# Sample window values in three transfers, and a ring of six value-page pairs, in a hybrid decoder step on Trainium2

## The chip, the cores and the metric

The kernel runs on one core of one Trainium2 chip. The metric is the device time of one execution in microseconds (us); lower is better. Engines are named as in the profile: PE (TensorE matmul), PEld (its weight loads), DVE (VectorE), ACT (ScalarE), POOL (GpSimd) and SP (SyncE, which here does nothing but issue DMA transfers).

## The reference, cut to what matters

One decoder layer runs on a prompt of 512 tokens and on 8 sample sequences of one new token each. Half of the heads do sparse attention in three branches (compressed, selected blocks, sliding window), the other half differential attention. For the samples, keys and values of 2048 past tokens lie in 16 pages of 128 tokens per sequence, found through a page table. The sliding branch of a sample has its own buffer of 512 past rows; the new token's row is appended, the oldest falls out, and the updated buffer is an output:

```python
kw = jnp.concatenate([win_k, wk], axis=1)
vw = jnp.concatenate([win_v, wv], axis=1)
w_pos = P - wbuf + jnp.arange(wbuf + Q, dtype=jnp.int32)
o = _nsa_branches(q, q_rot, gate, q_pos, kc, vc, cmp_end, n_sel, sel_gather, kw, vw, w_pos)
return o, kw[:, -wbuf:], vw[:, -wbuf:]
```

The sample's attention output is a sum over its pages of weights times values (128 tokens x 640 value columns a page: 512 for the differential heads, 128 for the selected branch), plus the compressed and the sliding branch. Then follow the output projection, a convolutional FFN and the final norm.

## The kernel before

The middle of the program (306 to 477 us of the profiled execution) is attention. Generators, one for each activity, yield operations with an estimated cost, and a planner in the kernel's Python (`Issue`) lays them in one order for each engine: at every step it takes, among the operations that could start soonest, the most urgent one by a plan that eight rehearsals refine. A number that a generator yields by itself is a pause: its next operation may not start earlier. The planner counts a transfer's result as usable 2.0 us after its end, and each ring of buffers as one more condition. Its order is fixed when the program is built; on the chip every engine runs its own instructions in that order and waits by semaphores. All transfers go through SP's one queue.

These generators matter here:

- `p_main` runs the prompt's attention in 12 units: `p_qk` (scores on PE, L423), `p_exp` (row minimum on DVE at L1828, exponential on ACT into tiles `p0` to `p3` of 128 to 512 columns), `p_scale`, `p_turn` (transposes on PE at L1889), `p_parts` (copies into `pt`) and `p_pv`. The tiles `p0` to `p3` lie in rings of `NPR` buffers each.
- `p_vload` fetches the samples' value pages in 64 pairs (`vp`, 320 KB a page, issued at L523) into a ring of `NV` pairs. `p_v` consumes them on PE: for each sample 8 pairs against `Sd` and `Ss`, then the sliding branch (`kcT` against `Sw`), then the next sample. A pair's buffer comes free when the `Ss` products of its group of two pairs are done.
- `p_win` brings the sliding branch's values of sample b into half of the tile `kcT` (two samples alternate): the whole 128 x 4 x 128 block (L2036), in which the last row holds a value that isn't wanted; then the new row from `vn` over row 127 of its last quarter (L2038), which marks `E("win", b)`; then the store of the updated buffer (L2040). `p_v` waits for `E("win", b)` before it goes on to sample b + 1, and the load for sample b waits until sample b - 2 is done.

Out-projection, FFN (up from 510 to 790 us) and the down-projection follow in straight loops.

Of the kernel before, what the change touches and what calls it, by code (L numbers as in the profile page):

```python
# [412 lines left out]
def build(tc, T, plan, last):  # L413
    with tc.manual_schedule():
        _build(tc, T, plan, last)


def _build(tc, T, plan, last):
    nc = tc.nc
    te, ve, se, ge, sy = nc.tensor, nc.vector, nc.scalar, nc.gpsimd, nc.sync  # L420
# [4 lines left out]
    def act(out, in_, func=AF.Copy, **kw):  # L425
        se.activation(out=out, in_=in_, func=func, **kw)  # L426
# [20 lines left out]
    def flat(ap):  # L447
        return ap.rearrange("p a b -> p (a b)")
# [231 lines left out]
    def E(*key):  # L680
        return ev.setdefault(key, Event())
# [979 lines left out]
    def p_window():  # L1661
# [17 lines left out]
                       t[:, j * 128:(j + 1) * 128], b4 == 0, b4 == 3)  # L1679
            yield (("pe", 0.24, f), E("wm", b)) + ((ksl,) if b == 0 else ())  # L1680
        yield ("act", tact(256), lambda: act(flat(Sw), box["p"][:, 0:256])), ksl.done, E("Sw")
    NV = 5
    PL = {}


# [83 lines left out]
    def at(*args):  # L1769
        return PL["AT"](*args)  # L1770
# [1 line left out]


    PTR, DV, WR, TMP = Ring(6), Ring(2), Ring(4), Ring(1)
    NPR = (5, 5, 5, 5)
    PR = [Ring(n) for n in NPR]
    VS = Ring(NV)
    PB, PT, W, O = {}, {}, {}, {}
    wslots, vslots = {}, {}

    def v_load(i):
        t = PL["VR"]("vp", [128, 2, 640], F32, NV)
        for n in range(2):
            page(t[:, n], T["vpg"], 128 + 2 * i + n)
        vslots[i] = t
# [29 lines left out]
    def p_exp(i, g, qs, box, sl, wslot):  # L1815
# [4 lines left out]
        for q in qs:  # L1820
# [4 lines left out]
            def f():  # L1825
                if q == 0 and g == 0:
                    W[i] = at("w", [128, 6, 4], F32, 4)
                ve.tensor_tensor_reduce(out=x, in0=x, in1=cm[:, S - n:], scale=-SC, scalar=3e38, op0=OP.add, op1=OP.min,  # L1828
                                        accum_out=W[i][:, g, q:q + 1])
            yield (("dve", tdve(n), f, PS),) + ((wslot,) if first and q == 0 else ())  # L1830
        for q in qs:
# [4 lines left out]
            def f():  # L1836
                t = at(f"p{q}", [128, n], F32, NPR[q])
                act(t, xs[q], AF.Exp, bias=W[i][:, g, q:q + 1], scale=-1.0, accum_out=W[i][:, 2 + g, q:q + 1])
# [187 lines left out]
    def win(b):  # L2026
        return kcT[:, 4 * (b % 2):4 * (b % 2) + 4]

    def p_win():

        yield E("kcT", 1)
        yield E("vn")
        for b in range(B):
            if b > 1:
                yield E("vb", b - 2)
            yield ("dma", 0.75, lambda: sy.dma_start(out=win(b), in_=T["winv"][b])),  # L2036
            yield 5.0
            yield ("dma", 0.05, lambda: sy.dma_start(out=win(b)[127:128, 3], in_=vn[b:b + 1, 0])), E("win", b)  # L2038
            yield 4.0
            yield ("dma", 0.75, lambda: sy.dma_start(out=T["swv"][b], in_=win(b))),  # L2040

    def p_v():
# [115 lines left out]
    def p_wo_first():  # L2158
# [12 lines left out]
        for m in range(2):  # L2171
            slots = [VS.slot() for _ in range(2)]
            for sl in slots:
                yield sl
                sl.got.t = -50.0
            h, l = prep["o", m] = [PL["VR"]("vp", [128, 2, 640], F32R, NV).rearrange("p a b -> p (a b)")[:, 0:1024]
                                   for _ in range(2)]
# [64 lines left out]
    for f, prio in ((p_stage2(), 0), (p_load(), 0), (p_w1v(), 0), (p_split(), 1), (p_product(), 3), (p_group("k"), 2), (p_group("v"), 2), (p_scores(), 2), (p_wload(), -1), (p_window(), 1),  # L2242
                    (p_turned(), 5), (p_vn(), 5), (p_nsa(0), 1), (p_nsa(1), 1), (p_cmp_sample(0), 1),
                    (p_cmp_sample(1), 1), (p_switch(), 0), (p_outs(), -3),
                    (p_vload(), 0), (p_win(), -1), (p_main(), 3),
                    (p_values(), 2), (p_pc(), 2), (p_seq(p_scale, range(NU)), 1),
                    (p_seq(p_turn, range(NU)), 1), (p_seq(p_pv, range(NU)), 0),
                    (p_seq(p_dv, [i for i in range(NU) if units[i][0] == "d"]), 3),
                    (p_seq(p_finish, [i for i in range(NU) if units[i][0] != "s"]), 1), (p_v(), v_prio),
                    (p_wo_first(), 4),  # L2250
                    (p_wo(), 4),
                    (p_out(0, 0, VB, "v"), 7)):
        Q.spawn(f, prio)
# [296 lines left out]
```

## Time and profile before

| | us |
|---|---|
| median of 3 runs | 950.04 (948.54 to 950.15) |
| the profiled execution's own time | 948.83 |
| its span, first to last instruction | 947.1 |
| share of the span in which PE is busy | 96% |
| attention with value pages being loaded | 329.6 to 461 |

The profile is of one execution, 1.2 us below the median of the runs; 1.7 us of its time lie outside the span. A busy PE isn't a PE at its peak: matmuls overlap, and their ends are modelled. An idle time in brackets names the event that ended it.

### The profile page before, as it was taken

The numbers are of one execution on the slowest core, as the hardware profiler recorded it, in microseconds if no ns is written. First come the engines' busy times: TensorE is split into PE (matmuls) and PEld (weight loads), VectorE is DVE, ScalarE is ACT, GpSimd is POOL, SyncE is SP. The second block draws the span as 40 slices with busy tenths as digits, with TensorE's granted clock in tenths as the row PEclk, the third lists the DMA queues.
The fourth block names the chain that finished last, engine by engine and source line by source line (L and its number), as shares of the span: only waits on it lengthen the run. The fifth ranks groups of instructions, "written<-read, shape, count | busy, mean of one in ns | idle before, by whom it ended". The sixth has DMA issues, their size and how long they took to land.

```text
span 947.1 us, 22410 instructions
## 1 busy us (share of the span) xinstructions
PE 911.7 (96%) x8628; PEld 813.8 (86%) x8628; DVE 579.2 (61%) x1396; ACT 383.9 (41%) x801; POOL 281.3 (30%) x377
## 2 busy tenths in 40 slices
PE   8999999999999889999998999999999999999995
PEld 5998888799999655655568999999999999999995
DVE  7786663356777766758854357777777777421234
ACT  5275422355555556545552234444444333211220
POOL 4120210000111000000105656666666666313230
PEclk9999999999999999999989999999999999999998
DMA  7669999977673698889714422222222222433322
GB/s 258 233 221 339 354 350 337 338 261 246 222 242 118 223 341 322 322 301 339 262 61 147 157 78 90 89 90 90 90 89 90 90 90 84 139 108 107 111 73 91
DMA packets 86059, 179.82 MB, mean 190 GB/s; under 512 B 10049, under 2 KB 28994, under 8 KB 85954
## 3 DMA queue, kind: packets, MB, share of 16 engines
q1 hardware_dynamic: 85954, 178.41, 54.7%
q8 instruction: 68, 1.11, 0.5%
q14 instruction: 37, 0.30, 0.1%
HBM read 165.78 MB, written 12.59 MB: 188 GB/s over the span
## 4 chain that ended last, share of the span: by engine, by line
PE 64%; DVE 19%; ACT 7%; issue 5%; DMA 4%; SPq 1%; POOL 1%; DVEq 0%; ACTq 0%; POOLq 0%
PE bank L423 60%; DVE c L435 12%; ACT c L426 4%; PE bank L1889 2%; DMA vp<-in_vpg 2%; DVE u L438 2%; DVE h L438 1%; DVE hl L432 1%; ACT hh L426 1%; ACT wh L426 1%; DMA kcT<-vn 1%; DMA cp<-in_cpg 1%; SPq L523 1%; POOL wl L432 0%; DVE rsm L435 0%
## 5 line engine op out<-in xcount | busy, mean ns | idle before, releaser
L423 PE MATMUL bank<-gh,wl 128*128 128x260 f32 x704 | 200.9, 285 | 3.3 <-POOL wl L432 3.3
L423 PE MATMUL bank<-gh,wh 128*128 128x260 f32 x704 | 199.1, 283 | 0.0
L423 PE MATMUL bank<-gl,wh 128*128 128x260 f32 x704 | 199.1, 283 | 0.0
L432 POOL TENSOR_TENSOR wl<-wr,wh 128x1024 fp32r<-128x1024 f32 x53 | 127.0, 2397 | 162.0 <-ACT wh L426 162.0
L426 ACT ACTIVATE wh<-wr 128x1024 fp32r<-128x1024 f32 (+2 forms) x95 | 97.2, 1023 | 157.5 <-PE bank L423 125.5
L435 DVE SCALAR_TENSOR_TENSOR c<-u,cvw,c 128x536 f32<-128x536 f32 x88 | 122.3, 1390 | 59.0 <-ACT c L426 57.4
L423 PEld LDWEIGHTS bank<-gh,wl 128*128 128x128 f32 x704 | 132.5, 188 | 6.9 <-POOL wl L432 6.9
L423 PEld LDWEIGHTS bank<-gl,wh 128*128 128x128 f32 x704 | 132.6, 188 | 0.0
L423 PEld LDWEIGHTS bank<-gh,wh 128*128 128x128 f32 x704 | 132.3, 188 | 0.1
L423 PE MATMUL bank<-xh,wh 128*128 128x260 f32 (+1 forms) x368 | 105.5, 289 | 1.1 <-ACT wh L426 1.1
L423 PE MATMUL bank<-xl,wh 128*128 128x260 f32 (+1 forms) x368 | 104.4, 286 | 1.7 <-DVE xl L435 1.6
L432 DVE TENSOR_TENSOR wl<-wr,wh 128x1024 fp32r<-128x1024 f32 (+2 forms) x41 | 52.7, 1285 | 81.0 <-ACT wh L426 80.1
L423 PE MATMUL bank<-xh,wl 128*128 128x260 f32 x352 | 100.0, 284 | 0.0
L423 PE MATMUL bank<-hh,wh 128*128 128x260 f32 (+2 forms) x340 | 96.4, 283 | 0.0
L423 PE MATMUL bank<-hl,wh 128*128 128x260 f32 (+2 forms) x340 | 96.1, 283 | 0.0
L423 PE MATMUL bank<-hh,wl 128*128 128x260 f32 (+2 forms) x340 | 96.1, 283 | 0.0
L423 PEld LDWEIGHTS bank<-xh,wh 128*128 128x128 f32 (+1 forms) x368 | 68.8, 187 | 6.8 <-issue 4.5
L423 PEld LDWEIGHTS bank<-xl,wh 128*128 128x128 f32 (+1 forms) x368 | 68.8, 187 | 2.7 <-DVE xl L435 2.7
L423 PEld LDWEIGHTS bank<-xh,wl 128*128 128x128 f32 x352 | 66.9, 190 | 0.0
L432 DVE TENSOR_TENSOR wl<-cp,wh 128x256 fp32r<-128x256 f32 x126 | 47.2, 433 | 28.8 <-ACT wh L426 27.4
L423 PEld LDWEIGHTS bank<-hh,wh 128*128 128x128 f32 x340 | 64.1, 189 | 0.0
L423 PEld LDWEIGHTS bank<-hh,wl 128*128 128x128 f32 x340 | 64.1, 188 | 0.0
(389 smaller groups left out, 1984.9 us busy)
## 6 DMA issues: line engine op xcount, KB each, us to landing
vp<-in_vpg SPq DMA_DIRECT2D x128, 320.0 KB, 5.4
kp<-in_kpg SPq DMA_DIRECT2D x128, 256.0 KB, 5.2
cp<-in_cpg SPq DMA_DIRECT2D x128, 192.0 KB, 4.2
wr<-in_w_up SPq DMA_DIRECT2D x44, 512.0 KB, 3.2
wr<-in_w_in SPq DMA_DIRECT2D x21, 512.0 KB, 5.1
wr<-in_w_down SPq DMA_DIRECT2D x16, 512.0 KB, 3.5
out_zT<-z SPq DMA_DIRECT2D x14, 260.0 KB, 5.5
wr<-in_w_down SPq DMA_DIRECT2D x8, 384.0 KB, 3.1
```

Of the source, the lines that this page charges most:

```text
L423: te.matmul(out, l, r, start=start, stop=stop)
L426: se.activation(out=out, in_=in_, func=func, **kw)
L432: eng.tensor_tensor(out=out, in0=a, in1=b, op=OP.subtract)
L435: ve.scalar_tensor_tensor(out=out, in0=a, scalar=s, in1=b, op0=o0, op1=o1, **kw)
L438: eng.tensor_tensor(out=out, in0=a, in1=b, op=op)
L523: sy.dma_start(out=dst, in_=src[bass.ds(numbers[k][i - k], 1)].rearrange("o p f -> (o p) f"))
L1889: te.transpose(p[:, j * 128:(j + 1) * 128], PB[i, g, q][0][:, k * 128:(k + 1) * 128], ident)
```

## The change

Three edits. The ring of value pages gets six pairs instead of five (5 KB more of each partition), and the ring of `p3`, the 512-column tile, four buffers instead of five (2 KB less). In `p_win` the load leaves out the last row: one transfer for the first three quarters of the block (128 rows of 1.5 KB), one for the first 127 rows of the last quarter (512 bytes each), and the new row goes out right behind them as a third, without the pause of 5.0 and in one operation that the planner takes to cost 1.2. The pause ahead of the store is 12.0 instead of 4.0. Since the planner orders everything by these figures, the order of all engines in attention is laid anew.

```diff
-    NV = 5
+    NV = 6
...
-    NPR = (5, 5, 5, 5)
+    NPR = (5, 5, 5, 4)
...
-            yield ("dma", 0.75, lambda: sy.dma_start(out=win(b), in_=T["winv"][b])),
-            yield 5.0
-            yield ("dma", 0.05, lambda: sy.dma_start(out=win(b)[127:128, 3], in_=vn[b:b + 1, 0])), E("win", b)
-            yield 4.0
+            w = win(b)
+
+            def f():
+                sy.dma_start(out=w[:, 0:3], in_=T["winv"][b][:, 0:3])
+                sy.dma_start(out=w[0:127, 3], in_=T["winv"][b][0:127, 3])
+                sy.dma_start(out=w[127:128, 3], in_=vn[b:b + 1, 0])
+            yield ("dma", 1.2, f), E("win", b)
+            yield 12.0
             yield ("dma", 0.75, lambda: sy.dma_start(out=T["swv"][b], in_=win(b))),
```

## Rows read from the trace of the kernel before

**Rows 1.** The page of the whole execution: busy time by engine, then PE and the DMA engines in 40 equal slices of the span, in tenths.
```profile
PE 911.7 (96%) x8628; PEld 813.8 (86%) x8628; DVE 579.2 (61%) x1396; ACT 383.9 (41%) x801; POOL 281.3 (30%) x377
...
PE   8999999999999889999998999999999999999995
...
DMA  7669999977673698889714422222222222433322
```

**Rows 2.** Stretches of attention: start and end, length, busy us of each engine (and instructions), granted clock, mean busy share of the 16 DMA engines, GB/s.
```profile
306.00:329.60 23.60, 21.16 (x209) 15.63 (x208) 17.93 (x71) 13.71 (x46) 0.48 (x1) 0.93 0.66 228
329.60:461.00 131.40, 125.18 (x1759) 77.07 (x1749) 93.55 (x352) 69.40 (x215) 6.01 (x7) 0.99 0.91 322
461.00:477.00 16.00, 13.71 (x159) 9.15 (x159) 13.60 (x55) 10.57 (x28) 5.29 (x4) 0.90 0.56 191
...
335.00:345.00 10.00, 9.17 (x140) 5.20 (x144) 8.98 (x36) 7.35 (x28) 1.50 (x2) 1.00 1.03 391
```

**Rows 3.** What PE waited for from 329.6 to 461 us (releaser, us in total, times, the longest), and from PE's order of time the instruction after the longest of these waits: start, length, what, count, in brackets the idle time ahead of it and what ended it.
```profile
PE bank L423 <- DMA vp<-in_vpg: 5.1, 8, 1.5
...
350.70 0.43 PE L423 MATMUL bank<-vp,Sd 128*32 128x128 f32 x8 [1.53 <-DMA vp<-in_vpg]
```

**Rows 4.** The granted clock in the two stretches of attention that follow an idle time of PE (columns as in rows 2).
```profile
350.99:354.41 3.42, 3.42 (x40) 2.29 (x29) 0.00 (x0) 1.65 (x4) 0.00 (x0) 0.50 1.06 407
473.87:480.69 6.82, 5.71 (x23) 3.54 (x23) 6.02 (x27) 6.10 (x17) 1.82 (x2) 0.50 0.16 57
```

**Rows 5.** What SP's queue waited for from 329 to 462 us: issuing line, releaser, us in total, times, the longest.
```profile
SPq L523 <- PE bank L423: 36.3, 24, 6.4
SPq L2040 <- DMA kcT<-vn: 7.4, 4, 2.3
...
SPq L2038 <- DMA kcT<-in_winv: 1.9, 3, 0.9
```

**Rows 6.** SP's issues in order of time: start, length of the group, line, transfer, count. The first five pairs and the first window load, then parts of the cycles of samples 0, 1 and 4.
```profile
306.42 0.88 SPq L523 DMA_DIRECT2D vp<-in_vpg  x2
...
309.08 4.33 SPq L523 DMA_DIRECT2D vp<-in_vpg  x8
...
322.62 0.42 SPq L2036 DMA_DIRECT2D kcT<-in_winv  x1
329.65 7.41 SPq L523 DMA_DIRECT2D vp<-in_vpg  x12
...
347.44 0.42 SPq L2040 DMA_DIRECT2D out_swv<-kcT  x1
348.44 0.88 SPq L523 DMA_DIRECT2D vp<-in_vpg  x2
349.42 0.49 SPq L2036 DMA_DIRECT2D kcT<-in_winv  x1
...
398.38 0.42 SPq L2036 DMA_DIRECT2D kcT<-in_winv  x1
...
401.52 8.83 SPq L523 DMA_DIRECT2D vp<-in_vpg  x12
410.39 0.56 SPq L2038 DMA_DIRECT2D kcT<-vn  x1
```

**Rows 7.** PE around the sliding branch's products (`kcT`,`Sw`) of sample 4, as the second row of rows 3.
```profile
417.01 0.30 PE L423 MATMUL bank<-kcT,Sw 128*32 128x128 f32 x1 [0.30 <-DMA kcT<-vn]
```

**Rows 8.** DMA in 329.6 to 461 us: packets; the queue's packets, MB and share of 16 engines; issues with KB each and median us to landing.
```profile
DMA packets 19140, 42.33 MB, mean 322 GB/s; under 512 B 2317, under 2 KB 2317, under 8 KB 19119
...
q1 hardware_dynamic: 19119, 42.04, 89.9%
...
vp<-in_vpg SPq DMA_DIRECT2D x118, 320.0 KB, 5.4
out_swv<-kcT SPq DMA_DIRECT2D x7, 256.0 KB, 4.8
kcT<-in_winv SPq DMA_DIRECT2D x7, 256.0 KB, 4.4
z<-in_w_out SPq DMA_DIRECT2D x1, 256.0 KB, 4.0
kcT<-vn SPq DMA_DIRECT2D x8, 0.5 KB, 5.9
```

**Rows 9.** DMA in 225 to 300 us, where most transfers have rows of 1.5 KB: the queue's packets, MB and share of 16 engines.
```profile
q1 hardware_dynamic: 10565, 15.03, 62.0%
```

**Rows 10.** The exponentials of 512 columns as a group (ACT, 320 to 480 us: count, busy us, mean ns, idle ahead of them), then the two on ACT and the two turns on PE that stand closest.
```profile
L426 ACT ACTIVATE p<-bank,w 128x512 f32<-128x512 f32 x24 | 16.4, 685 | 16.6 <-DVE w L1828 13.6 <-DVE w L1850 2.9
...
391.72 0.68 ACT L426 ACTIVATE p<-bank,w 128x512 f32<-128x512 f32 x1
...
392.60 0.69 ACT L426 ACTIVATE p<-bank,w 128x512 f32<-128x512 f32 x1
...
392.02 0.55 PE L1889 MATMUL bank<-cst,p 128*128 128x128 f32 x3
...
393.29 0.98 PE L1889 MATMUL bank<-cst,p 128*128 128x128 f32 x7
```

**Rows 11.** PE at the end of attention, as the second row of rows 3.
```profile
473.50 0.74 PE L557 MATMUL bank<-cst,rsm 128*128 128x128 f32 x4 [1.18 <-DVE w L1850]
...
475.57 1.09 PE L1889 MATMUL bank<-cst,p 128*128 128x128 f32 x4 [1.06 <-DVE t L435]
```

## The prediction

> **What bounds the kernel now.** I read the page first, then attention by stretches, then what PE and SP wait for in it, then the transfers. The page shows PE busy nearly from end to end, and the one place with both PE and the DMA engines near their limit: slices 14 to 20, attention with value pages [rows 1]. By stretches, 329.6 to 461 us has PE busy 125.2 of 131.4 us and each DMA engine busy 0.91 of the time; what follows needs few transfers [rows 2]. So PE sets the time, and only its idle time and its slow clock can be won back; the DMA engines are the runner-up, with some 13 us to spare in 131.
>
> In that stretch PE stands idle 6.2 us. 5.1 of these end with the landing of a value page, in eight places, the longest 1.53 us ahead of 350.70 [rows 3]. Right behind that one the granted clock is 0.50, the lower of the two levels (1.2 GHz), for 3.4 us from 350.99; it is so again for 6.8 us from 473.87, where PE waits on DVE [rows 4]. At half the clock 3.4 us of matmuls do 1.7 us of work, so the wait at 350 may have cost up to 1.7 us more.
>
> SP waits 36.3 us for PE to free page buffers, 7.4 for the new row to land ahead of the store, and 1.9 for the load to land ahead of the row [rows 5]. Its order of issues shows why the sliding branch matters: for sample 4 the load goes out at 398.38, but the row only at 410.39, behind twelve page issues of the sort that wait for buffers [rows 6]. PE reaches sample 4's sliding product and waits the last 0.30 us for that row, at 417.01, 6.6 us after its issue [rows 7]. Only then does `p_v` go on to sample 5. So pages are held until the row is there, then eaten in a burst, and the ring runs dry behind the burst.
>
> **The change part by part.** *Six pairs.* The sixth pair's load hangs on the release one pair earlier. Five pairs (ten pages) are out by 313.4, and no page follows until 329.65 [rows 6]. One more pair (640 KB) moves into that gap: at 322 GB/s that is 2.0 us of transfers less in the stretch. Later, each pair is asked for one pair earlier, that is 131.4/59 = 2.2 us earlier on average, more than the longest single wait of 1.53. If the engines keep up, all 5.1 us of waits go, and perhaps the 1.7 us of slow clock: a gain between 0 and 6.8 us.
>
> *Row beside the load.* SP no longer waits 1.9 us between load and row, and with 12.0 us of pause the store meets a row that has landed (median 5.9 us after its issue [rows 8]), so its 7.4 us go too. What queues behind these waits on SP are page issues; SP has 36.3 us of waits for buffers to absorb them, so by itself this is worth 0. There is one more issue for each sample, 8 x 0.42 us of SP, hidden under the same 36.3 us. If SP weren't waiting for buffers, both would show as pages issued that much earlier or later.
>
> *The 127 rows.* Here I see the cost. The stretch has 133 large transfers of 128 rows and eight new rows, and 2317 packets under 512 bytes: 16.4 for each of the 141 [rows 8]. So I read each transfer as cut into 16 equal shares, 8 rows to an engine, each closed by one tiny packet. 127 rows have no equal cut but into one share. No row here shows a transfer of 127, so the ends are these. In 16 unequal shares an engine gets 8 rows of 512 bytes, under 0.3 us, nothing. In one share, all 65 KB pass through one engine. An engine moved 322/16/0.91 = 22.1 GB/s while busy [rows 2], which makes 2.9 us by bytes. The mean packet took 131.4 x 16 x 0.899/19119 = 98.9 ns at 2199 bytes [rows 8], and 75 x 16 x 0.620/10565 = 70.4 ns at 1423 bytes [rows 9]; the line through both gives 37 ns at 512 bytes, 4.7 us for 127. (At the full 98.9 ns it would be 12.6, but the two means show that small packets are cheaper.) I take one share, since the packets speak for equal shares, and 3.5 us, nearer to the price by bytes, because both means hold the closing packets.
>
> The Trainium skill (DMA: Bandwidth & Descriptors, "Why a DMA increments its semaphore by 16 and not by 1") says that a transfer is spread over the largest number of engines up to 16 that divides its slowest dimension, so 128 partitions use 16 and 127 use one. The count of closing packets agrees with the first half; no run here shows the second. By that rule the sum is the one below; without it the first rival's.
>
> The queue is in order on each engine, so that engine's share of every page behind the 127 rows is late by as much, and a page is there only when all its shares are. One sample's load gets shorter by a quarter, 65 KB over 16 engines, 0.2 us. Net 3.3 us for each sample on one engine. Sample 0's falls at 322, when the stretch hasn't begun; seven are left: +23.1 us. That engine had 131.4 x 0.899 = 118.1 us of work; with the sixth pair's 1.9 us moved ahead it has 139.3, against 131.4 us of stretch: +7.9 if it is never idle and its packets cost what they did. Part of that price is crowding: from 335 to 345 us, share 1.03 moved 391 GB/s, 7% more for each busy us than the mean [rows 2]. At that price 116.2 shrinks to 108.3, and the sum is 131.4: +0. The other fifteen engines will be idle more, so the price falls, but the busy one can't be without gaps. I take the middle, +4.0. Today's waits for pages are inside the 131.4, so the ring's gain isn't subtracted again: it goes into the queue that this engine forms.
>
> *Four `p3` buffers.* Read in the order of before, 22 of the 24 exponentials of 512 columns start after the turn that would free the buffer four back. The two of unit 5 don't: 391.72 would wait for the turn that ends at 392.57, 392.60 for the one that ends about 393.8, three of the seven transposes from 393.29 [rows 10]. So 0.9 and 1.2 us on ACT, which is idle 47% of the stretch; their results are turned long after. Cover gone, 2.1 us. I take 0.
>
> *The new order.* Page pairs weigh 1.95 and each window 1.2 + 0.75 in the planner, which knows nothing of the slow engine. What a fresh order is worth no row shows; I leave it at 0 and widen the range by 2 us.
>
> *The end of attention.* PE idles 1.18 and 1.06 us for DVE behind the last pages [rows 11]. If PE comes to that place later, DVE is further ahead: -0.5.
>
> **Sum.** +4.0 - 0.5 = +3.5 us: 948.83 of the profiled execution becomes 952.3. That execution lies 1.2 below the median of the runs, and a median is predicted: 953.5, slower.
>
> **Rivals.** *The engines keep up, and the kernel is faster.* One mechanism: the 127 rows occupy no single engine for long. The engines have 13.3 us to spare, and 1.9 from the moved pair; shared among seven samples that is 2.2 us, and below this price nothing is paced. Then the 5.1 us of waits go and part of the 1.7; DVE and ACT, 71% and 53% busy, take back some: -4.5, 945.5. For it: all eight waits are shorter than a pair's lead. Against it: the closing packets.
>
> *No change.* PE's waits move to other pages and stay at some 5 us, the busy engine just keeping step: 950 within 1.9 us. The +0 end of the sum above is this.
>
> *The row isn't sent beside the load.* If the third transfer, or the store of the other half, were taken for a writer of the same place, SP would stand through the load's 4.4 us [rows 8] once a sample. For halves the trace speaks against it: sample 1's load goes out at 349.42, 2 us after sample 0's store [rows 6], which takes 4.8 to land. For rows of one column range nothing is shown. Seven stands are 31 us of SP; its waits for buffers would hide most of them. With a third left on the path, an estimate, 10 us: 960.
>
> **How the numbers follow.** A difference under 0.2% (1.9 us) can't be told from none here. One engine paces: 0.50, its own range 949.5 to 962 (the +0 end, less the 0.5; the +7.9 end with half of the 8.4 that 4.7 us a sample would add), of which 0.05 lie within 0.2%. Engines keep up: 0.30, 943 to 948.5, 0.02 within. No change: 0.15. SP stands: 0.05. So faster 0.28, same 0.22, slower 0.50. The range from 944 to 962 leaves out the best of the second case and the worst of the first.
>
> **What would show it.** Right: in the stretch with value pages, GB/s falls below 322 while waits of PE for value pages grow past 5.1 us, most of them on pages issued just behind a window load; SP's waits for the row vanish; landings of the 127 rows lie 3 us and more above the 5.9 of today's row. Wrong: pages land as before, waits for them are under 2 us, and the half-clock stretch at 351 is gone. A wait on `kcT` ahead of the third transfer would show the third rival; exponentials of 512 columns waiting for turns would show that four buffers are too few.

## The result, and the profile after

The changed kernel takes 961.43 us (median of 5 runs, 958.73 to 962.01) against 950.04 before: ratio 1.0117, 95% interval 1.0088 to 1.0147, or 11.1 us more (8.4 to 14.0). Slower, as forecast, but by three times the 3.5 us of the sum. Below, a ratio is always against runs of the kernel before on the same chip, and microseconds worked out from it are the ratio's distance from 1 times 950. The profiled execution of the changed kernel took 962.01 us, 0.6 above the median. One execution of kernel 9 that took 2592.89 us is left out of its ratio.

The page after, beside [rows 1]: busy time by engine, and the DMA engines in 40 slices.

```profile
PE 916.8 (95%) x8628; PEld 814.5 (85%) x8628; DVE 581.2 (61%) x1400; ACT 383.6 (40%) x797; POOL 283.5 (30%) x377
...
DMA  7659999984874698887743522222222222333322
```

PE still works nearly throughout. From the start of the span to the first product of the FFN, which comes at 541.53 us before and at 555.10 us after, the stretches read (before, then after; columns as in [rows 2]):

```profile
0.00:541.53 541.53, 520.75 (x5421) 427.71 (x5421) 351.64 (x1022) 253.22 (x640) 81.15 (x136) 0.97 0.75 261
```

```profile
0.00:555.10 555.10, 526.40 (x5420) 428.68 (x5421) 353.77 (x1026) 252.88 (x636) 83.37 (x136) 0.97 0.75 255
```

All of the loss lies ahead of the FFN: 13.6 us there, and 13.0 in the whole span (960.1 against 947.1). PE's idle time grows from 541.53 - 520.75 = 20.8 us to 555.10 - 526.40 = 28.7, so 7.9 are new waits; the other 5.7 are the same products taking longer. Attention by stretches, beside [rows 2]:

```profile
306.00:331.00 25.00, 22.15 (x205) 19.65 (x204) 14.78 (x50) 13.19 (x39) 2.41 (x7) 0.86 0.62 221
331.00:461.00 130.00, 120.19 (x1634) 74.22 (x1634) 90.40 (x342) 67.25 (x211) 8.67 (x8) 0.95 0.84 282
461.00:491.50 30.50, 30.00 (x363) 17.62 (x361) 25.03 (x91) 18.28 (x50) 4.65 (x3) 1.00 0.74 255
```

In the long stretch the transfers fell from 322 to 282 GB/s and the DMA engines from 0.91 to 0.84, while PE idles 9.8 of 130 us (before 6.2 of 131.4). Value pages now last until 491.5. What PE waited for from 331 to 491.5 us, beside [rows 3], and five places in order of time:

```profile
PE bank L423 <- DMA vp<-in_vpg: 3.1, 2, 2.7
PE bank L423 <- DMA kcT<-vn: 2.2, 2, 1.4
PE bank L557 <- DVE rsm L435: 1.5, 1, 1.5
...
PE bank L423 <- DMA kcT<-in_winv: 0.6, 1, 0.6
```

```profile
340.17 1.44 PE L423 MATMUL bank<-vp,Sd 128*32 128x128 f32 x16 [2.72 <-DMA vp<-in_vpg]
383.96 0.42 PE L423 MATMUL bank<-kcT,Sw 128*32 128x128 f32 x6 [0.57 <-DMA kcT<-in_winv]
385.73 0.27 PE L423 MATMUL bank<-kcT,Sw 128*32 128x128 f32 x1 [1.35 <-DMA kcT<-vn]
...
400.83 0.98 PE L557 MATMUL bank<-cst,rsm 128*128 128x128 f32 x4 [1.50 <-DVE rsm L435]
...
404.07 0.60 PE L423 MATMUL bank<-kcT,Sw 128*32 128x128 f32 x2 [0.83 <-DMA kcT<-vn]
```

Waits for pages shrank from 5.1 to 3.1 us; waits for the window and its row came in their place, 2.8 against 0.3. The granted clock, beside [rows 4], in two stretches:

```profile
339.50:346.30 6.80, 6.00 (x56) 2.90 (x56) 1.91 (x6) 1.35 (x5) 0.00 (x0) 0.50 0.96 323
401.00:407.80 6.80, 5.97 (x24) 2.41 (x22) 4.57 (x21) 2.58 (x9) 1.27 (x1) 0.50 0.84 280
```

The first of them begins within the wait of 2.72 us for a page. The second begins behind the 1.50 us for `rsm` from DVE; the wait for the window's row lies inside it and can't have brought it on.

SP is where the new thing stands. Its waits from 329 to 482 us (beside [rows 5]), its issues of windows over the whole run (nanoseconds, minimum, median, maximum), and one cycle in order of time (beside [rows 6]):

```profile
SPq L523 <- PE bank L423: 33.4, 19, 5.5
...
SPq L2041 <- DMA vp<-in_vpg: 1.7, 3, 0.9
```

```profile
L2040 SPq DMA_DIRECT2D kcT<-in_winv x8: 290/328/506, 322.3 to 473.3; - x8
L2041 SPq DMA_DIRECT2D kcT<-vn x8: 3365/3922/4224, 323.1 to 473.6; - x8
```

```profile
356.10 0.40 SPq L2039 DMA_DIRECT2D kcT<-in_winv  x1
356.59 0.29 SPq L2040 DMA_DIRECT2D kcT<-in_winv  x1
356.94 4.22 SPq L2041 DMA_DIRECT2D kcT<-vn  x1
361.41 12.97 SPq L523 DMA_DIRECT2D vp<-in_vpg  x16
```

The transfers from 330 to 480 us, beside [rows 8] (KB each, median us to landing):

```profile
vp<-in_vpg SPq DMA_DIRECT2D x114, 320.0 KB, 5.2
...
kcT<-in_winv SPq DMA_DIRECT2D x7, 63.5 KB
kcT<-vn SPq DMA_DIRECT2D x7, 0.5 KB, 7.4
```

SP's waits for row and load are gone from the list. But issuing the row, 512 bytes, holds SP for 3.9 us where it took 0.56 before [rows 6]. Ahead of three of the seven in this stretch a wait for a landing page is listed, 0.9 us at most; the 3.9 us are not in any wait. The eight issues come to some 31 us in which no page goes out. They are called stands below.

What ends a stand can be read from the single packets in the trace. The 127 packets of 512 bytes move one behind the other, 23.5 ns apart and 3.0 us in all, and SP comes free 0.1 to 0.4 us after the first of them starts. That holds for all 40 stands at the row in the changed kernel and in kernels 6, 9, 11 and 12 below. For the stand at 356.94 the packets start at 360.96. The DMA engines up to there, and in the 1.4 us behind it (columns as in [rows 2]):

```profile
356.94:360.96 4.02, 4.02 (x42) 1.76 (x40) 3.92 (x18) 3.34 (x12) 0.61 (x1) 1.00 0.88 310
360.96:362.36 1.40, 1.40 (x10) 0.61 (x8) 0.61 (x3) 0.65 (x3) 0.00 (x0) 1.00 0.13 38
```

So the queue empties while SP stands, and then little but the 127 rows moves: in the 1.4 us behind the start of the packets the mean busy share lies between 0.08 and 0.36 for the eight samples.

### The profile page after: what moved, and what is told of

Its sections match the earlier page's. It is cut to its first block, busy times and chain, and to the rows that moved or that the text cites. A ratio compares the mean times of both kernels' runs of the same rounds, so it can differ in the third digit from the quotient of the medians.

```text
span 960.1 us, 22424 instructions
## 1 busy us (share of the span) xinstructions
PE 916.8 (95%) x8628; PEld 814.5 (85%) x8628; DVE 581.2 (61%) x1400; ACT 383.6 (40%) x797; POOL 283.5 (30%) x377
## 4 chain that ended last, share of the span: by engine, by line
PE 59%; DVE 20%; DMA 7%; ACT 6%; issue 4%; SPq 2%; POOL 0%; ACTq 0%; DVEq 0%; POOLq 0%
PE bank L423 56%; DVE c L435 12%; ACT c L426 4%; DMA vp<-in_vpg 2%; PE bank L1889 2%; SPq L523 2%; DVE u L438 2%; DMA cp<-in_cpg 2%; DMA kcT<-vn 1%; DVE h L438 1%; DVE hl L432 1%; DMA kp<-in_kpg 1%; ACT hh L426 1%; ACT wh L426 1%; DMA wr<-in_w_in 1%
```

## The experiments

Two things can be at work: the transfers themselves, and the order, which the planner lays anew as soon as one of its figures changes. Each was tried with the other held. The order of before is kept by leaving the planner's figures alone and changing only what an operation issues or how many buffers are allocated.

| kernel | order | median us | ratio (95%) | us |
|---|---|---|---|---|
| changed kernel | anew | 961.43 | 1.0117 (1.0088 to 1.0147) | +11.1 |
| 1: 112 + 15 rows | as the change | 957.4 | 1.0081 (1.0054 to 1.0108) | +7.7 |
| 2: window loaded whole | as the change | 961.16 | 1.0135 (1.0110 to 1.0160) | +12.8 |
| 3: 127 rows, row at its old place | before | 956.87 | 1.0078 (1.0051 to 1.0105) | +7.4 |
| 4: six pairs, four `p3` | before | 942.66 | 0.9929 (0.9906 to 0.9953) | -6.7 |
| 5: six pairs, four `p3` | anew | 952.77 | 1.0036 (1.0019 to 1.0054) | +3.4 |
| 6: window alone | anew | 967.01 | 1.0161 (1.0131 to 1.0191) | +15.3 |
| 7: four `p3` alone | anew | 950.3 | 0.9997 (0.9980 to 1.0015) | -0.3 |
| 8: a pause of 4.1 for 4.0 | anew | 949.33 | 0.9999 (0.9979 to 1.0019) | -0.1 |
| 9: the whole change | before | 958.24 | 1.0085 (1.0059 to 1.0111) | +8.1 |
| 10: the same, 112 + 15 rows | before | 946.37 | 0.9948 (0.9926 to 0.9969) | -4.9 |
| 11: the change, 28 rehearsals | anew | 954.5 | 1.0041 (1.0021 to 1.0061) | +3.9 |
| 12: the change, window counted ready later | anew | 951.94 | 1.0008 (0.9988 to 1.0029) | +0.8 |

**1, 127 rows as 112 and 15, in the order of the change.**

```diff
-                sy.dma_start(out=w[0:127, 3], in_=T["winv"][b][0:127, 3])
+                sy.dma_start(out=w[0:112, 3], in_=T["winv"][b][0:112, 3])
+                sy.dma_start(out=w[112:127, 3], in_=T["winv"][b][112:127, 3])
```

> The changed kernel with its order of instructions kept, and the 127 rows sent as two transfers of 112 and 15 rows, which both have a cut into many equal shares (one issue more for each sample, some 0.4 us of SP). The theory of the prediction (the 127 rows go through one engine and hold up what is queued behind them): with them gone the time falls from 961.4 to 945 to 951, and the issue of the new row, which takes SP about 4 us in the changed kernel, is back at 0.6 us. The rival (the new order of all engines costs the time, wherever the rows go): 958 to 962, though the row's issue gets short.

The row's issue fell back to 0.50 to 0.62 us, and PE no longer waited for a window at all. Yet only 3.4 us came back (0 to 7, from the two intervals), and 7.7 stay. The packets of the 112 + 15 rows move up to ten at once. So SP's stand comes from the 127 rows, and something else in the changed kernel costs too. The twelve executions of this kernel scatter widely, from 951.99 to 964.77 us.

**2, the window loaded whole in the order of the change.** The first three issues become one load of 128 rows with the row right behind it.

```diff
-                sy.dma_start(out=w[:, 0:3], in_=T["winv"][b][:, 0:3])
-                sy.dma_start(out=w[0:127, 3], in_=T["winv"][b][0:127, 3])
+                sy.dma_start(out=w, in_=T["winv"][b])
```

> The changed kernel with its order kept, but the window is loaded whole (128 rows of 2 KB, one transfer) and the new row follows right behind, so it has to wait on SP until the load has landed. Theory of the 127 rows: no engine is held up, but SP stands 4 to 6 us for each landing, so part of the cost stays: 950 to 957. Theory of the order: 958 to 962. If SP's standing is what costs (4 us of issue time in the changed kernel, 4 to 6 us of waiting here), the time equals that of the changed kernel or is 1 to 4 us above it.

+12.8 us. Here the row overwrites what the load writes, so SP has to wait for the load to land:

```profile
SPq L2040 <- DMA kcT<-in_winv: 45.3, 8, 7.0
```

This shows the third rival as it was meant. It isn't what the changed kernel does: there no such wait is listed. The time fits both rivals that were set out, the order and SP's standing, and doesn't tell them apart.

**3, 127 rows in the order of before, row at its old place, five pairs.**

```diff
-            yield ("dma", 0.75, lambda: sy.dma_start(out=win(b), in_=T["winv"][b])),
+            def f():
+                sy.dma_start(out=win(b)[:, 0:3], in_=T["winv"][b][:, 0:3])
+                sy.dma_start(out=win(b)[0:127, 3], in_=T["winv"][b][0:127, 3])
+            yield ("dma", 0.75, f),
```

> The kernel before with its order kept; only the window load is cut as in the change (three quarters, then 127 rows of the last), the new row stays at its old place behind the pause. Theory of the 127 rows: what is issued next behind them, a value page, takes SP about 4 us, seven or eight times, and pages land late: 954 to 962. Theory of the order: 950, within 2 us, as the order is that of before.

+7.4 us from the cut of the load alone. The row goes out later in this kernel, and its issue takes 0.51 to 0.63 us again; the stand falls on whatever follows the 127 rows closely. At sample 4 it is a load of a weight tile (SP in order of time; the packets start at 408.08):

```profile
405.54 0.34 SPq L2038 DMA_DIRECT2D kcT<-in_winv  x1
405.92 2.34 SPq L2171 DMA_DIRECT2D z<-in_w_out  x1
```

In the other cycles it is a value page, for 0.36 to 2.96 us. PE's waits for pages rose to 7.1 us.

**4, six pairs and four `p3` buffers in the order of before.**

```diff
-("vp", [128, 2, 640], F32, NV)
+("vp", [128, 2, 640], F32, 6)
...
-at(f"p{q}", [128, n], F32, NPR[q])
+at(f"p{q}", [128, n], F32, (5, 5, 5, 4)[q])
```

> The kernel before with its order kept instruction for instruction; only the buffers differ: six for value pages, four for the 512-column tile. By the rows of before the eight waits for pages (5.1 us) go, and the half-clock stretch at 351 us with them: 944 to 947. If the waits come from landings that a sixth buffer doesn't bring forward, or if four 512-column buffers hold up ACT: 949 to 952.

942.66 us, 6.7 less than before and the fastest kernel of all. PE's waits for pages from 329.6 to 480 us, and the stretch of [rows 2]:

```profile
PE bank L423 <- DMA vp<-in_vpg: 0.2, 1, 0.2
```

```profile
329.60:461.00 131.40, 127.94 (x1832) 80.21 (x1828) 97.22 (x366) 71.60 (x222) 6.49 (x7) 0.99 0.94 330
```

5.1 us of waits for pages became 0.2, and the half-clock stretch at 351 us is gone. Not all of it is won: PE now waits 2.0 us for DVE ahead of 337.39, which it didn't between 329.6 and 461 us in the kernel before, and a half-clock stretch follows.

```profile
PE bank L1577 <- DVE nsc L1569: 2.0, 1, 2.0
```

```profile
337.73:341.14 3.41, 3.41 (x29) 1.46 (x30) 2.31 (x9) 1.99 (x7) 0.00 (x0) 0.50 0.99 345
```

**5, the same counts, order planned anew.** The window is as before.

```diff
-    NV = 5
+    NV = 6
...
-    NPR = (5, 5, 5, 5)
+    NPR = (5, 5, 5, 4)
```

> The kernel before with two constants changed, the counts of buffers (six value-page pairs, four p3), so that the order is planned anew for them; the window is loaded whole, as before. With the order of before these counts gave 942.7 us. If a new order is as good as the old one on the mean: 941 to 945. If any new planning loses what the change's planning lost (some 8 to 14 us, by the 112 + 15 run): 950 to 957. If the loss comes from the window's new weights alone (1.2 and a pause of 12): 941 to 945 here and the loss in the run with the window alone.

952.77 us: with the same buffers the new order loses 10.2 us against kernel 4. Its value pages end as early (462.8 against 462.6 us), and the loss follows behind them. What PE waited for longest from there to the FFN, and the granted clock in that place:

```profile
PE bank L423 <- ACT p L426: 4.2, 1, 4.2
...
PE bank L1889 <- DVE o L435: 1.8, 1, 1.8
```

```profile
469.90:480.10 10.20, 9.22 (x36) 7.72 (x37) 6.81 (x23) 5.89 (x19) 3.85 (x3) 0.50 0.00 0
```

By these waits, softmax work of the prompt's attention stands at the end with no matmuls to cover it.

**6, the window alone, order planned anew.** The edit of `p_win` is the change's; the counts of buffers stay.

```diff
-            yield ("dma", 0.75, lambda: sy.dma_start(out=win(b), in_=T["winv"][b])),
-            yield 5.0
...
+            yield ("dma", 1.2, f), E("win", b)
+            yield 12.0
```

> The changed window alone (127 rows, new row beside them, weight 1.2, pause 12), five value-page pairs and five p3 buffers, order planned anew. 127 rows in the old order gave 956.9. If the planning is neutral: 955 to 959. If the window's weights spoil the order: 962 to 970, and products of the compress branch that end late, as after (330.7 us against 315.8).

967.01 us, the slowest. PE, 329.6 to 500 us:

```profile
PE bank L423 <- DMA kcT<-vn: 8.6, 6, 1.8
PE bank L423 <- DMA vp<-in_vpg: 2.8, 4, 2.0
...
PE bank L423 <- DMA kcT<-in_winv: 0.9, 1, 0.9
```

PE is sent to windows that haven't landed, and has five pairs only. The time lies in the range given for a spoilt order, but the sign named with it didn't come: the compressed branch's last products (with `w1vh`) start at 316.6 us, as against 315.3 before and 330.3 in the changed kernel.

**7 and 8, a new order without new work.** Four `p3` buffers alone (7), and the pause ahead of the store planned at 4.1 (8).

```diff
-    NPR = (5, 5, 5, 5)
+    NPR = (5, 5, 5, 4)
```

```diff
-            yield 4.0
+            yield 4.1
```

> The kernel before with four p3 buffers in place of five and nothing else; the order is planned anew. If four buffers are enough and the planning is neutral: 949 to 951. If the fourth count is what the exponentials of 512 columns wait for in the new order: 953 to 958, with ACT waiting for turns of p3.

> The kernel before with the pause ahead of the store planned at 4.1 in place of 4.0: no instruction is added, taken away or changed, only the order is planned anew. The difference to before is what a new order is worth by itself. If orders are alike: 949 to 951. If the planner's result scatters on the chip: anything from 944 to 958, and then the new order of the change needs no other cause than that.

Both stay where before is, at 950.3 and 949.33 us. Four buffers are enough, and in these two a new order costs nothing. They are smaller steps than the change's: PE's instructions differ from those of before in some 800 and 1050 of 8628 places of the order, and in some 2700 in the changed kernel.

**9, the whole change in the order of before.** Buffers as in kernel 4; the load's operation issues all three transfers, and the row's old operation is empty.

```diff
-            yield ("dma", 0.75, lambda: sy.dma_start(out=win(b), in_=T["winv"][b])),
+            def f():
+                sy.dma_start(out=w[:, 0:3], in_=T["winv"][b][:, 0:3])
+                sy.dma_start(out=w[0:127, 3], in_=T["winv"][b][0:127, 3])
+                sy.dma_start(out=w[127:128, 3], in_=vn[b:b + 1, 0])
+            yield ("dma", 0.75, f),
             yield 5.0
-            yield ("dma", 0.05, lambda: sy.dma_start(out=win(b)[127:128, 3], in_=vn[b:b + 1, 0])), E("win", b)
+            yield ("dma", 0.05, lambda: None), E("win", b)
```

> All the instructions of the change (127 rows, the row beside them, six value-page pairs, four p3 buffers) in the order planned for the kernel before; the row goes out with the load, the store at its old place. If the new order is what makes the change slow: 942.7 of the six pairs in that order plus 4 to 7 for the 127 rows, 946 to 951. If the parts don't add, because SP's stand behind the 127 rows and the six pairs need each other's slack: 955 to 961, and the order is not to blame.

**10, the same with 112 + 15 rows.**

```diff
-                sy.dma_start(out=w[0:127, 3], in_=T["winv"][b][0:127, 3])
+                sy.dma_start(out=w[0:112, 3], in_=T["winv"][b][0:112, 3])
+                sy.dma_start(out=w[112:127, 3], in_=T["winv"][b][112:127, 3])
```

> The same, with the 127 rows sent as 112 and 15. The order of before, six pairs, four p3 buffers, the row beside the load. If one engine's share and SP's stand are the whole price of the 127 rows: 941 to 944, as with six pairs alone. If the row beside the load is worth something by itself (no wait of SP between load and row, 1.9 us, nor ahead of the store, 7.4 us, and no sample's sliding product waiting for its row): 938 to 941. If 15 rows on another number of engines still cost: 944 to 947.

Kernel 9 takes 958.24 us, 8.1 more than before; kernel 10 takes 946.37, 4.9 less. They differ in one transfer. Its price, 1.0085/0.9948, is 13 us (10 to 16), nearly twice what it is in kernel 3. SP around sample 4, first kernel 9, then kernel 10:

```profile
400.52 0.28 SPq L2040 DMA_DIRECT2D kcT<-in_winv  x1
401.33 4.13 SPq L2041 DMA_DIRECT2D kcT<-vn  x1
...
406.34 5.97 SPq L523 DMA_DIRECT2D vp<-in_vpg  x9
```

```profile
400.39 0.51 SPq L2042 DMA_DIRECT2D kcT<-vn  x1
...
402.31 9.51 SPq L523 DMA_DIRECT2D vp<-in_vpg  x14
```

PE in kernel 9 just behind it; then the clock there and behind five short waits for pages (0.16 to 0.40 us each) at sample 2:

```profile
410.16 0.43 PE L423 MATMUL bank<-vp,Sd 128*32 128x128 f32 x8 [1.82 <-DMA vp<-in_vpg]
```

```profile
366.20:373.00 6.80, 6.80 (x56) 4.62 (x56) 3.76 (x15) 3.77 (x12) 0.00 (x0) 0.50 0.86 278
410.60:414.00 3.40, 3.04 (x27) 1.92 (x28) 0.00 (x0) 0.43 (x1) 0.00 (x0) 0.50 1.00 372
```

This is the mechanism in one place. The next pages go out 4.0 us later (406.34 against 402.31); 2.0 of these come with this stand, as the page ahead of it was 2.0 late already. The ring runs dry, PE waits 1.82 us, and the granted clock, which was at the higher level (2.4 GHz), falls to the lower (1.2 GHz) for 3.4 us. Over all the pages the lag adds up: the first goes out 1.6 us earlier in kernel 9 than in kernel 10, the last 6.9 us later.

The wait is paid twice here, as idle time and as slow clock: PE's 9.8 busy us at half the clock in these two stretches cost some 4.9, an estimate, beside 6.0 us of waits for pages. Kernel 10 has 1.5 us of such waits and no half-clock stretch between 325 and 478 us. Not every wait is paid twice: the wait for `nsc` that a half-clock stretch followed in kernel 4 stands in kernel 10 too, without one.

```profile
338.79 0.27 PE L1577 MATMUL bank<-cst,nsc 128*2 128x128 f32 x1 [2.05 <-DVE nsc L1569]
```

Two limits. The pages of the five waits at sample 2 were issued from 355.8 to 358.5 us, ahead of the stand at 362.86. What can bear on them is the stand before it, from 348.73 to 351.83: pages had been going out 2.9 us earlier than in kernel 10, and behind it only 1.0 to 1.7. And the profiled execution of kernel 9, 954.3 us, is one of its faster ones, so that only 6.9 us of the difference can be looked at in the two profiles.

Kernel 10 lies in the range given for a cost that is left with 15 rows, 944 to 947. But its difference from kernel 4, +1.8 us, is within its error of 3.0, so no such cost is shown.

**11, 28 rehearsals in place of 8.** The only edit to the changed kernel.

```diff
-REHEARSALS = 8
+REHEARSALS = 28
```

> The changed kernel with 28 rehearsals of the planning in place of 8: the best plan found ends 3.7 earlier by the planner's own count (473.2 against 477.0), below the 474.1 of before. If the order is slow because these eight rehearsals found only a poor plan: 947 to 954, about what the change gives in the order of before. If the planner's count doesn't tell what the chip does: 957 to 965.

**12, the window counted ready later.**

```diff
-            yield ("dma", 1.2, f), E("win", b)
-            yield 12.0
+            yield ("dma", 1.2, f),
+            yield 5.0
+            yield ("dma", 0.05, lambda: None), E("win", b)
+            yield 7.0
```

> The changed kernel, with the planner told that a window is ready 5 later than it believes in the change (5.8 behind the start of its load, as before, in place of 1.2; the pause ahead of the store is 7 in place of 12, its place in the plan the same). No instruction differs, only their order. If the order is slow because PE is sent to windows that haven't landed (it waited 2.2 us for rows and 3.7 for loads in the changed kernel): 950 to 956, and these waits gone. If those waits are a small part of it: 957 to 963.

Both have the change's instructions, 127 rows and all, in another order: 954.5 and 951.94 us, 7 and 10 less than the changed kernel. The first lies 0.5 above the range given for a better plan, the second within the one given for windows counted ready later. In kernel 12, PE's list from 318 to 480 us has no wait for a window any more:

```profile
PE bank L423 <- DMA vp<-in_vpg: 4.5, 13, 0.7
PE bank L423 <- ACT p L426: 2.8, 1, 2.8
PE bank L1889 <- ACT pt L426: 0.9, 3, 0.4
PE bank L423 <- DVE w L1850: 0.8, 1, 0.8
```

The 3.7 us for loads that the expectation names were waits of PE's weight loads, which overlap PE; PE itself waited 0.6.

The change moves the pause from ahead of the mark `E("win", b)` to behind it. So the planner counts a window as ready 1.2 + 2.0 = 3.2 us behind the start of its load, where before it was 0.75 + 5.0 + 0.05 + 2.0 = 7.8; in the changed kernel the row lands 7.4 us behind the start of its own issue (median). Kernel 11 still waits 4.1 us for rows and 3.0 for windows, and is faster all the same, so these waits aren't all of what an order can cost.

## Why the prediction was right in sign and short in size

The measured 961.43 lies 0.6 us inside the range of 944 to 962. That is partly luck: the 127 rows and the new order both cost more than was taken for them, and only the width left for the worst case held the two.

**The cut of the load: right place, wrong size.** This was the step that carried the sum, and it is what makes the change slow in the order of before: +8.1 us (5.6 to 10.5, kernel 9). The prediction took +4.0, between +0 and +7.9. The term that was mis-sized has two causes.

First, it let one DMA engine fall behind and the other fifteen go on. What the traces show is one step earlier: SP can't issue the next transfer until the 127 rows begin to move, the pages behind go out later, and by then all the engines have little left to do (0.88 of the time, then 0.13, around 360.96 us). The pages then land about as fast as before, median 5.2 us after their issue in the changed kernel and 5.6 in kernel 9, against 5.4 [rows 8]. That was one of the prediction's marks of being wrong, and it came. An added issue was priced at 0.42 us, hidden under SP's waits for buffers; with the stand it is, by the medians, 0.42 + 2.7 a sample in kernel 9 and 0.42 + 3.4 in the changed kernel. Had these waits absorbed it, they would have shrunk by the stands. They didn't: from 329 to 462 us they are 20.1 us in kernel 9 and 14.8 in kernel 10, which has no stands.

That all 127 rows go through one engine was right, as far as their packets tell, which move one behind the other. The Trainium skill (DMA: Bandwidth & Descriptors, "Why a DMA increments its semaphore by 16 and not by 1") would put 127 rows on one engine, 112 on sixteen and 15 on fifteen. The runs agree: the packets of the 127 rows move singly, while those of 112 + 15 up to ten at once in kernel 1 and eleven in kernel 10. The 127 take 3.0 us, the 2.9 that the prediction had by bytes, and not the 3.5 that it took. The stand is of a like length, 1.4 to 5.1 us, but it isn't the time of their passage: it is over when they start.

Second, the slow clock behind the waits was left out of this term, although it was counted for the waits of before [rows 4]. In the profile of kernel 9 it is some 4.9 us, beside 4.5 us of further waits for pages; other places give part of it back.

**Six pairs: right.** The gain alone is 6.7 us (4.5 to 8.9), at the top of the 0 to 6.8 given. Part of the agreement is luck: in kernel 4 the new wait for `nsc` and the half-clock stretch behind it took some back, the half-clock stretch at the end of attention shrank from 6.8 us to 3.4 (from 474.26), and neither was foreseen. Beside the 127 rows it is gone: kernel 9 against kernel 3, which also sends the row at another place, is +0.7 us within 3.5. That it "goes into the queue" and isn't to be subtracted was the right reading, and so was the first rival: without the 127 rows the kernel would be faster (kernel 10).

**The row beside the load, four `p3` buffers: right.** Kernel 10 against kernel 4 is +1.8 us within 3.0, and kernel 7 is -0.3 within 1.7. Neither can be told from 0, which was the value taken for both.

**The new order: taken as 0 with 2 us either way, and this was too narrow.** For the change as a whole it comes to +3.0 us within 3.7 (changed kernel against kernel 9). But the same instructions lie 10 us apart in four orders (958.24, 961.43, 954.5, 951.94), and six pairs alone lose 10.2 us in theirs. Nor do the two causes add. In the order of before the 127 rows cost 13 us; in the order of the change 3.4. The order costs 12.6 us without them (kernel 1 against 10), and 3.0 with them. It seems that an order that sends PE to pages or windows too early and a queue that delivers them late lose partly the same time; this isn't shown further. Counted in the order of before, -6.7 (pairs) + 1.8 (row) + 13.0 (127 rows) + 3.0 (order) is the 11.1 measured; each is the difference of two of these kernels, one step further each time, so they have to add up.

Part of what the change's order loses lies ahead of the first window load at 321 us. From 24 to 300 us PE idles 5.1 to 5.6 us in the three kernels that have this order (the changed one, 1 and 2), and 2.0 to 3.5 in the eleven others (before, then after):

```profile
24.00:300.00 276.00, 273.35 (x2666) 251.58 (x2665) 176.22 (x447) 123.95 (x287) 30.93 (x92) 0.99 0.81 276
```

```profile
24.00:300.00 276.00, 270.45 (x2621) 244.27 (x2620) 171.80 (x440) 119.33 (x273) 29.24 (x84) 0.99 0.82 278
```

The compressed branch's last products with `w1vh` start at 330.3 us in the changed kernel and at 314.5 and 314.6 in kernels 12 and 11, which are faster with the same instructions.

**The end of attention: -0.5.** The two waits of [rows 11], 1.18 and 1.06 us, aren't there any more: from 414 to 520 us PE waits nowhere longer than 0.50 us, and from 461 to 491.5 us the granted clock is 1.00. But the work is laid elsewhere by the new order, and waits for `w` (0.8 us) and `rsm` (1.5) stand at 366.40 and 400.83 instead. The reason given, that PE comes to that place later, isn't tested.

**The third rival** named the right place, SP standing at the row, and the nearest time, 960, with a chance of 0.05. Its reason was wrong: SP doesn't wait for the load to land (kernel 2 does, 45.3 us in all). The stand comes from the 127 rows ahead, and goes when they are sent as 112 and 15 (kernel 1).

**Its own marks.** GB/s below 322: yes, 282. SP's waits for the row gone: yes. Waits for pages past 5.1 us: in kernels 3 and 9 (7.1 and 6.0), not in the changed kernel (3.1), where waits for the window took their place. Pages landing as before, a mark of being wrong: yes, 5.2 us against 5.4. Landings of the 127 rows aren't recorded; the row's own grew from 5.9 to 7.4 us, its long issue included.

**What stays open.** Why SP stands until the 127 rows begin to move: the traces show when a stand ends, not its cause. Why this plan is slow beyond its waits for windows: of the 5.7 us by which PE's busy time grew ahead of the FFN, 3.5 fall on the products against `Qzs` (14.5 to 18.0 us), ahead of the value pages; half-clock stretches give some 0.6 of the 5.7 (PE is busy 25.9 us in them before and 27.2 after), and the rest wasn't traced to a cause. And whether a longer search would always find a good order: by the planner's own count, which is no time of the chip, the plans of kernels 12, 11 and the changed one end at 472.3, 473.2 and 477.0, the same sequence as on the chip; three plans are too few to rely on it.

## What to carry to other kernels

Cutting a transfer from 128 rows to 127 can hold up the queue for the next issue: 1.4 to 5.1 us here, against 0.5, and cutting it again into 112 and 15 takes this away. Where an order is planned from figures, change the buffers with the order held first: six pairs were worth 6.7 us in the old order and lost 3.4 in a new one. When an operation's pause is moved, look at which mark the planner hangs on it, for it moves when consumers are sent.

## What the runs showed of the hardware that wasn't expected

The issue of a 512-byte transfer took 3365 to 4224 ns right behind one of 127 rows of 512 bytes in the changed kernel (1.4 to 5.1 us over five kernels), and 502 to 621 ns behind 112 + 15 rows. It was over 0.1 to 0.4 us after the first of the 127 packets had started, while the packets went on, one by one, for 3.0 us. With another transfer in that place, it was that one that stood (2.34 us for a weight tile). The stand shows in no list of waits, only in the duration of the issue.
